# Gate and up of a SwiGLU feed-forward in seven half-size products instead of eight, with two accumulator tiles read in turn

## The chip, the cores and the metric

One core of one Trainium2 chip. Its engines run side by side, each with a queue of its own that is worked off in order: TensorE (PE; PEld is its weight load), VectorE (DVE), ScalarE (ACT), GpSimd (POOL) and SyncE (SP, which here issues most transfers). TensorE writes its sums into PSUM, of which the feed-forward uses four tiles of two banks in turn; everything else lies in SBUF. The metric is the device time of one execution in microseconds; less is better.

## The reference

One inference step of a small decoder trunk: a Conformer convolution layer, then a layer of dilated sliding-window attention, each followed by a SwiGLU feed-forward, for 512 prompt columns and 64 sample columns. The change concerns the feed-forward, which is computed twice:

```python
def swiglu(x, g, w_gate_up, w_down):
    gu = rms_norm(x, g) @ w_gate_up
    return (jax.nn.silu(gu[..., :D_FF]) * gu[..., D_FF:]) @ w_down
```

D_MODEL is 1024 (8 tiles of 128), D_FF is 2816 (22 blocks of 128). All values are fp32.

## The kernel before

Activations stand transposed: 128 partitions hold a tile of the model dimension, and the N = 576 columns are the tokens. A matmul takes a column half of 288 (HN). To keep fp32 accuracy, each operand is split into a high part (rounded, format fp32r) and a low part (the rest), and each product of two tiles is three matmuls: high by high, high by low, low by high (`mm3`, L227 to L230).

`ffn` (L772) works in two halves of 11 blocks. For each block f it computes gate and up: `proj` (L274) runs 8 tiles of the model dimension x 2 column halves x 3 matmuls for gate (48 matmuls) and the same for up, so 96 in a block, into one PSUM tile each. Behind it DVE multiplies with the row scale rs (L795), ACT takes silu (L797), DVE multiplies up with rs (L799) and with the gate (L800), and the result is split into hh (ACT, L271) and hl (DVE, L272). After 11 blocks come the down products of that half: 8 output tiles with 11 x 2 x 3 = 66 matmuls each, which DVE adds into the residual xT (L810). The very first block computes gate and up as a `pair` (L284), which alternates between two PSUM tiles every three matmuls, because its input arrives tile by tile.

Weights stream in: `w_load` (L110) issues the transfer of a block's weights (1 MB for gate and up) from SP into one of two raw buffers; `w_split` (L130) makes high (ACT, L140) and low parts (DVE, L141) into one of two pairs of buffers whi and wlo; `w_next` (L161) hands out what is ready, loads the block after next and splits the next. `bg_copy` (L180) issues at each `w_next`, on the same SP queue, one or two background copies of 1 MB from cache to output. The order of all instructions is the program's own: each engine works them off as they were written, and semaphores hold back what isn't ready. After the first feed-forward, `x_fill` (L848) prepares the attention's input behind each of the last down products; after the second, `y_rows` (L1546) transposes and writes the output.

Of the kernel before, what the change touches and what calls it, by code (L numbers as in the profile page):

```python
# [44 lines left out]
GH = 3072  # L45
DFF = 2816
FT = DFF // 128
TAPS = 31
EPS = 1e-6
SC = HD ** -0.5  # L50
# [40 lines left out]
def trunk(ctx: ExitStack, tc: tile.TileContext, I, O, dbg=None):  # L91
# [12 lines left out]
    def spec(ap, shape, scale=None):  # L104
        specs.append((ap, shape, scale))

    wstate = {"raw": [], "ready": [], "n": 0, "rate": 1.5, "lo": nc.vector, "cut": 4}
    BUFR, BUFH = 2, 2

    def w_load():  # L110
        if not specs:
            return
        ap, shape, scale = specs.pop(0)
        raw = wpool.tile([128, WSLOT], F32, tag="wraw", name="wraw", bufs=BUFR)
        n = int(np.prod(shape))
        v = raw[:, :n]
        if len(shape) == 2:
            v = v.rearrange("p (a b) -> p a b", a=shape[0])
        else:
            v = v.rearrange("p (a b c) -> p a b c", a=shape[0], b=shape[1])  # L120
        if len(shape) == 2:
            nc.sync.dma_start(v, ap)
        else:
            for j in range(shape[1]):
                nc.sync.dma_start(v[:, :, j], ap[j])
        wstate["raw"].append((raw, n, shape, scale))

    parts = []

    def w_split(cut=None):  # L130
# [5 lines left out]
        hi = wpool.tile([128, WSLOT], F32R, tag="whi", name="whi", bufs=BUFH)  # L136
        lo = wpool.tile([128, WSLOT], F32R, tag="wlo", name="wlo", bufs=BUFH)

        def plain(c):
            nc.scalar.activation(hi[:, c], raw[:, c], AF.Copy)  # L140
            wstate["lo"].tensor_sub(lo[:, c], raw[:, c], hi[:, c].bitcast(F32))  # L141

        def scaled(k, m):
            c = slice(k * m, (k + 1) * m)
            nc.scalar.activation(hi[:, c], raw[:, c], AF.Copy, scale=scale[:, k:k + 1])
            nc.vector.scalar_tensor_tensor(lo[:, c], raw[:, c], scale[:, k:k + 1],
                                           hi[:, c].bitcast(F32), op0=ALU.mult, op1=ALU.subtract)

        if scale is None:
            parts.extend(partial(plain, slice(i * n // cut, (i + 1) * n // cut)) for i in range(cut))  # L150
        else:
            parts.extend(partial(scaled, k, n // shape[0]) for k in range(shape[0]))
        pat = "p (a b) -> p a b" if len(shape) == 2 else "p (a b c) -> p a b c"
        kw = dict(a=shape[0]) if len(shape) == 2 else dict(a=shape[0], b=shape[1])
        wstate["ready"].append((hi[:, :n].rearrange(pat, **kw), lo[:, :n].rearrange(pat, **kw)))

    def w_work(n=100):
        for _ in range(min(n, len(parts))):
            parts.pop(0)()

    def w_next(lazy=False):  # L161
        w_work()
# [32 lines left out]

    def ffn_specs(l):
        wg, wd = I["w_gate_up"][l], I["w_down"][l]
        for hf in range(2):
            for f in range(hf * 11, hf * 11 + 11):
                spec([col_blocks(wg, 0, KT, f * 128, 128), col_blocks(wg, 0, KT, DFF + f * 128, 128)], (KT, 2, 128))  # L200
            for m in range(KT):
                spec(col_blocks(wd, hf * 11, 11, m * 128, 128), (11, 128))

    ffn_specs(0)

# [75 lines left out]
                    j == 0, j == len(ks) - 1)  # L281
        return pt[:, :, :HN]

    def pair(ps, wh, wl, xh, xl):  # L284

        pts = [ps.tile([128, 2, 512], F32, tag="mm", name="pmp") for _ in range(2)]
        for k in range(KT):
            for h in range(2):
                c = slice(h * HN, (h + 1) * HN)
                for i in range(2):  # L290
                    mm3(pts[i][:, h, :HN], wh[i][:, k], wl[i][:, k], xh[:, k, c], xl[:, k, c], k == 0, k == KT - 1)
        return pts

    def cut2(w):
# [477 lines left out]
    def ffn(l, u, before_last, after, late=0):  # L772
        with ExitStack() as cx:
            big = cx.enter_context(tc.tile_pool(name=f"f_big{l}", bufs=1))
            wk = cx.enter_context(tc.tile_pool(name=f"f_wk{l}", bufs=2))
            ps = cx.enter_context(tc.tile_pool(name=f"f_ps{l}", bufs=4, space=PSUM, reuse_waits="tile"))
            rs = big.tile([128, N], F32, name="rs")
            hh = big.tile([128, 11, N], F32R, name="hh")
            hl = big.tile([128, 11, N], F32R, name="hl")
            ks = [(k, k) for k in range(KT)]  # L780
            for hf in range(2):
                for f in range(11):
                    wh, wl = w_next()
                    if hf == 0 and f == 0:

                        pg, pu = (x[:, :, :HN] for x in pair(ps, [wh[:, :, i] for i in range(2)],
                                                             [wl[:, :, i] for i in range(2)], u.uh, u.ul))
                    else:
                        pg = proj(ps, wh, wl, u.uh, u.ul, ks, lambda w, k: w[:, k, 0])
                        pu = proj(ps, wh, wl, u.uh, u.ul, ks, lambda w, k: w[:, k, 1])  # L790
                    if hf == 0 and f == 0:
                        rstd_bc(ps, wk, u.acc, rs)
                        nc.scalar.activation(u.acc[:, 0:1], u.acc[:, 0:1], AF.Silu)
                    t = wk.tile([128, N], F32, name="gt")
                    nc.vector.tensor_mul(halves(t), pg, halves(rs))  # L795
                    s = wk.tile([128, N], F32, name="sg")
                    nc.scalar.activation(s, t, AF.Silu)  # L797
                    t2 = wk.tile([128, N], F32, name="gt2")
                    nc.vector.tensor_mul(halves(t2), pu, halves(rs))  # L799
                    nc.vector.tensor_mul(t2, t2, s)  # L800
                    split(hh[:, f], hl[:, f], t2)
                if hf:
                    u.close()
                    before_last()
                for m in range(KT):
                    wh, wl = w_next()
                    pt = proj(ps, wh, wl, hh, hl, [(k, k) for k in range(11)], lambda w, k: w[:, k])
                    if hf and late and m:
                        after(ps, wk, m - 1)
                    nc.vector.tensor_add(halves(xT[:, m]), halves(xT[:, m]), pt)  # L810
                    if hf and not late:
                        after(ps, wk, m)
                if hf and late:
                    after(ps, wk, KT - 1)


# [780 lines left out]
```

## Time and profile before

| | |
|---|---|
| Median of 3 runs (lowest, highest) | 2047.7 us (2044.57, 2049.89) |
| The profiled execution: its time | 2048.85 us |
| Its span, and its granted TensorE clock | 2047.1 us, 0.983 |
| TensorE matmul busy | 1948.9 us (95%), 17109 records |
| DVE, ACT, POOL busy | 1013.2, 810.2, 158.8 us |
| First feed-forward | about 305 to 718 us |
| Second feed-forward | about 1625 to 2041 us |
| Main transfer queue | 384.06 MB, 62.7% of 16 engines |

How to read it: a row of instructions names the line, the engine, the operation, output<-inputs and the shape; then the count, the busy time, the mean length of one and the idle time in front of them with what ended it. Matmuls overlap in TensorE's pipeline, so the length of one is more than their distance. A window's row gives each engine's busy time and count in that stretch, then the granted clock, the share of the transfer engines and GB/s.

### The profile page before, as it was taken

What the parts mean: (1) busy time and instruction counts of PE and PEld (TensorE: products, weight loads), DVE (VectorE), ACT (ScalarE), POOL (GpSimd) and SP (SyncE); (2) the same over time, 40 slices, a digit from 0 to 9 for tenths busy, and PEclk for the clock granted to TensorE, in tenths of its full rate; (3) what the DMA queues carried; (4) which work ended last, traced back from release to release, by engine and by line L of the source; (5) the groups of instructions that cost most, each with busy time, mean ns of one, the idle gap of its engine ahead of it and who ended that gap; (6) DMA issues with size and microseconds to landing.
All of it is one profiled execution on the core that took longest, in us unless ns stands there. A gap on an engine that the chain in (4) does not pass through costs nothing.

```text
span 2047.1 us, 40767 instructions
## 1 busy us (share of the span) xinstructions
PE 1948.9 (95%) x17109; PEld 1799.7 (88%) x17109; DVE 1013.2 (49%) x1922; ACT 810.2 (40%) x1836; POOL 158.8 (8%) x292
## 2 busy tenths in 40 slices
PE   6989699999999999999999999989988999999998
PEld 6767499999999999988888888877667999999998
DVE  5766674433343477356356445524556444334432
ACT  6554643221222344444244434437764332112221
POOL 1000000000000033032022012200113000000000
PEclk9999799999999999999999999999988999999999
DMA  7440086658665866787986986989686665633222
GB/s 212 144 145 23 23 295 217 225 210 279 206 205 185 294 207 181 238 233 192 252 226 187 258 253 198 217 213 229 176 191 214 208 209 199 234 97 83 77 72 75
DMA packets 368874, 387.82 MB, mean 189 GB/s; under 512 B 17983, under 2 KB 357975, under 8 KB 367010
## 3 DMA queue, kind: packets, MB, share of 16 engines
q1 hardware_dynamic: 368130, 384.06, 62.7%
q8 instruction: 135, 2.21, 0.5%
q0 software_dynamic: 560, 1.14, 0.2%
q14 instruction: 49, 0.40, 0.1%
HBM read 348.07 MB, written 146.86 MB: 242 GB/s over the span
## 4 chain that ended last, share of the span: by engine, by line
PE 88%; ACT 4%; DVE 3%; DMA 3%; issue 1%; SPq 1%; another core or an unknown queue 0%; ACTq 0%; DVEq 0%
PE pmm L230 13%; PE pmm L229 13%; PE pmm L228 13%; PE pj L228 7%; PE pj L229 7%; PE pj L230 7%; PE pj L1192 3%; PE tp L965 3%; PE acc L558 3%; PE pmp L229 2%; PE pmp L230 2%; PE pmp L228 2%; PE pv L1063 2%; PE tp L990 2%; ACT prod L588 1%; PE sc L1328 1%
## 5 line engine op out<-in xcount | busy, mean ns | idle before, releaser
L230 PE MATMUL pmm<-uh,wlo 128*128 128x288 f32 x1344 | 396.2, 295 | 0.0
L228 PE MATMUL pmm<-uh,whi 128*128 128x288 f32 x1344 | 395.9, 295 | 0.0
L229 PE MATMUL pmm<-ul,whi 128*128 128x288 f32 x1344 | 395.8, 294 | 0.0
L228 PE MATMUL pj<-whi,xh 128*128 128x256 f32 x1152 | 332.8, 289 | 0.9 <-DVE xT L810 0.9
L229 PE MATMUL pj<-wlo,xh 128*128 128x256 f32 x1152 | 321.8, 279 | 0.0
L230 PE MATMUL pj<-whi,xl 128*128 128x256 f32 x1152 | 321.8, 279 | 0.0
L228 PEld LDWEIGHTS pmm<-uh,whi 128*128 128x128 f32 x1344 | 252.1, 188 | 0.1
L229 PEld LDWEIGHTS pmm<-ul,whi 128*128 128x128 f32 x1344 | 252.1, 188 | 0.1
L230 PEld LDWEIGHTS pmm<-uh,wlo 128*128 128x128 f32 x1344 | 252.1, 188 | 0.0
L228 PEld LDWEIGHTS pj<-whi,xh 128*128 128x128 f32 x1152 | 216.3, 188 | 11.4 <-issue 10.8
L140 ACT ACTIVATE whi<-wraw 128x1024 fp32r<-128x1024 f32 (+3 forms) x206 | 169.2, 871 | 123.1 <-PE pmm L229 100.6
L229 PEld LDWEIGHTS pj<-wlo,xh 128*128 128x128 f32 x1152 | 216.5, 188 | 0.0
L230 PEld LDWEIGHTS pj<-whi,xl 128*128 128x128 f32 x1152 | 216.0, 187 | 0.0
L141 DVE TENSOR_TENSOR wlo<-wraw,whi 128x1024 fp32r<-128x1024 f32 (+3 forms) x206 | 197.7, 1003 | 23.7 <-ACT whi L140 23.4
L228 PE MATMUL pmm<-hh,whi 128*128 128x288 f32 x704 | 207.6, 295 | 0.0
L230 PE MATMUL pmm<-hh,wlo 128*128 128x288 f32 x704 | 207.5, 295 | 0.0
L229 PE MATMUL pmm<-hl,whi 128*128 128x288 f32 x704 | 207.2, 294 | 0.0
L799 DVE TENSOR_TENSOR gt<-pmm,rs 128x576 f32<-128x576 f32 x42 | 31.8, 757 | 224.6 <-PE pmm L230 224.6
L271 ACT ACTIVATE hh<-gt 128x576 fp32r<-128x576 f32 x44 | 30.2, 686 | 263.3 <-DVE gt L800 263.3
L229 PEld LDWEIGHTS pmm<-hl,whi 128*128 128x128 f32 x704 | 132.1, 188 | 0.0
L228 PEld LDWEIGHTS pmm<-hh,whi 128*128 128x128 f32 x704 | 132.1, 188 | 0.0
L230 PEld LDWEIGHTS pmm<-hh,wlo 128*128 128x128 f32 x704 | 132.0, 188 | 0.0
(295 smaller groups left out, 3516.4 us busy)
## 6 DMA issues: line engine op xcount, KB each, us to landing
out_dram<-in_cache_kv_w_dram SPq DMA_DIRECT2D x64, 1016.0 KB
wraw<-in_w_gate_up_dram SPq DMA_DIRECT2D x88, 512.0 KB
out_dram<-in_cache_kv_w_dram SPq DMA_DIRECT2D x32, 1008.0 KB
wraw<-in_w_kv_dram SPq DMA_DIRECT2D x24, 1024.0 KB
wraw<-in_w_down_dram SPq DMA_DIRECT2D x32, 704.0 KB
kk<-in_cache_kv_w_dram SPq DMA_DIRECT2D x40, 512.0 KB
vv<-in_cache_kv_w_dram SPq DMA_DIRECT2D x40, 512.0 KB
scr<-r SPq DMA_DIRECT2D x36, 512.0 KB
```

Of the source, the lines that this page charges most:

```text
L140: nc.scalar.activation(hi[:, c], raw[:, c], AF.Copy)
L141: wstate["lo"].tensor_sub(lo[:, c], raw[:, c], hi[:, c].bitcast(F32))
L228: nc.tensor.matmul(out, wh, xh, start=start, stop=False)
L229: nc.tensor.matmul(out, wh, xl, start=False, stop=False)
L230: nc.tensor.matmul(out, wl, xh, start=False, stop=stop)
L271: nc.scalar.activation(hi, x, AF.Copy)
L558: nc.tensor.matmul(acc[r][32 * (j - m):32 * (j - m) + 32], DG[c][g, j], exf[c][g, j:S + j], start=m == 0, stop=j + 4 >= TAPS)
L799: nc.vector.tensor_mul(halves(t2), pu, halves(rs))
L965: nc.tensor.transpose(pt[:, j * 128:(j + 1) * 128], Z["k", n][:, j, i * 128:(i + 1) * 128], ident)
L990: nc.tensor.matmul(pt[32 * bi:32 * bi + 32, a:a + n], q[:, x, i, b], kn[:, x, i, T * b:T * b + T] if k is None else k[:, i, bi], start=i = ...
L1063: nc.tensor.matmul(pvt[r], ph[:n, ti, r], v[:n, bi], start=i == 0, stop=i == 9)
L1192: nc.tensor.matmul(pt[:, :CW], xs[:, k], x[:, k], start=k == 0 and x is wh, stop=k == KT - 1 and x is wl)
```

## The change

The inner dimension (8 tiles) is halved, the 576 columns are halved, and gate and up are the two halves of the output: a 2 x 2 by 2 x 2 block product. Before, it takes 8 half-size products (4 tiles x 3 = 12 matmuls each); Winograd's form of Strassen's scheme needs 7, at the price of sums of the weights (four, `sw`), sums of the inputs (four, `th` and `tl`) and sums of the results.

- The 22 blocks are worked in quarters of 5, 6, 6 and 5 (`QUARTERS`). The first quarter stays as it was (`plain`, L869), since the row scale rs is known only after its first block. Since gate and up columns of both halves are mixed, the inputs must carry rs beforehand: `input_sums` (L844) makes the four scaled sums behind blocks 1 to 4, and `rescale` (L857) rewrites the parts of uh and ul that are used directly, during the first quarter's down products.
- In the other 17 blocks `seven` (L891) issues the seven products into two PSUM tiles: pwa (one bank, a) and pwc (two banks, c and b), in the order a, c, a, b, a, c, a. Several products add onto what stands in the bank; in between ACT copies the bank's state (p1, p5, u2, u3) or DVE reads it, while the next product goes to the other tile.
- The weights of such a block are seven parts of 512 columns, in two buffers of whi and wlo: r0, r1 and two sums, then two sums and r3. `w_split` queues the four sums (DVE, L193), then two splits of 1024 columns (L314, L315); `w_tail` (L134) makes the rest, after the block that uses the second buffer has ended. The raw buffer is free only after that.
- The down products come after each quarter, with 5 or 6 tiles inside, in pairs of output tiles (640 or 768 columns of weights a part); the first pair of each quarter runs as `pair`.

The core of the diff:

```diff
+QUARTERS = [(0, 5), (5, 6), (11, 6), (17, 5)]
...
+    def w_tail():
...
+            split(hi[:, :1024], lo[:, :1024], sw[:, 1024:])
+            split(hi[:, 1024:1536], lo[:, 1024:1536], raw[:, 1536:])
...
+            parts.extend([partial(add, t[0], r[2], r[3]), partial(sub, t[1], t[0], r[0]), partial(sub, t[2], r[0], r[2]),
+                          partial(sub, t[3], r[1], t[1]), direct, summed])
...
+            def input_sums(j):
...
+                nc.vector.tensor_sub(t[:, 0], za[:, h1], za[:, h0])
+                nc.vector.tensor_sub(t[:, 1], zb[:, h1], t[:, 0])
+                nc.vector.tensor_sub(t[:, 2], zb[:, h1], za[:, h1])
+                nc.vector.tensor_sub(t[:, 3], zb[:, h0], t[:, 1])
+                nc.scalar.activation(th[:, :, j], t, AF.Copy)
...
+            def seven(i):
+
+                wxh, wxl, wyh, wyl = w_take()
+                pa = ps.tile([128, 2, 512], F32, tag="mm", name="pwa")
+                pc = ps.tile([128, 2, 512], F32, tag="mm", name="pwc")
+                a, b, c = pa[:, 0, :HN], pc[:, 1, :HN], pc[:, 0, :HN]
...
+                direct(a, wxh, wxl, 0, 0, h0, True)
+                nc.scalar.activation(sn["p1"], a, AF.Copy)
+                summed(c, wxh, wxl, 2, 0, True)
+                nc.scalar.activation(sn["p5"], c, AF.Copy)
+                if sums_next:
+                    w_split()
+                    w_work(4)
+                summed(a, wxh, wxl, 3, 1, False)
+                nc.scalar.activation(sn["u2"], a, AF.Copy)
+                direct(b, wxh, wxl, 1, 4, h0, True)
+                nc.vector.tensor_add(s[:, h0], sn["p1"], b)
+                flush()
+                if not sums_next:
+                    w_split()
+                w_work(1)
+                nc.scalar.activation(s[:, h0], s[:, h0], AF.Silu)
+                summed(a, wyh, wyl, 0, 2, False)
+                nc.scalar.activation(sn["u3"], a, AF.Copy)
+                nc.vector.tensor_add(t2[:, h1], sn["u3"], sn["p5"])
+                w_work()
+                direct(c, wyh, wyl, 1, 4, h1, False)
+                nc.vector.tensor_add(s[:, h1], sn["u2"], c)
+                nc.scalar.activation(s[:, h1], s[:, h1], AF.Silu)
+                summed(a, wyh, wyl, 2, 3, False)
+                nc.vector.tensor_mul(t2[:, h1], t2[:, h1], s[:, h1])
+                nc.vector.tensor_mul(t2[:, h0], s[:, h0], a)
+                w_tail()
+                nc.scalar.activation(hh[:, i], t2, AF.Copy)
+                pend.append(lambda: nc.vector.tensor_sub(hl[:, i], t2, hh[:, i].bitcast(F32)))
+                if not sums_next:
+                    flush()
```

**DVE in one gate block.** Before, of one block in the second half of the first feed-forward (a gt with a number is the product of gate and up):

```order
L795 TENSOR_TENSOR gt<-pmm,rs 128x576
L799 TENSOR_TENSOR gt_5282<-pmm,rs 128x576
L800 TENSOR_TENSOR gt_5282<-gt_5282,sg 128x576
L272 TENSOR_TENSOR hl<-gt_5282,hh 128x576
L141 TENSOR_TENSOR wlo<-wraw,whi 128x1024 x2
```

Now, of one half-size block (p and u with numbers are ACT's copies; two of the four weight sums of line 193 stand ahead of the first row):

```order
L193 TENSOR_TENSOR sw<-wraw 128x512
L193 TENSOR_TENSOR sw<-wraw,sw 128x512
L925 TENSOR_TENSOR sg<-p_4736,pwc 128x288
L943 TENSOR_TENSOR hl<-gt_4615,hh 128x576
L315 TENSOR_TENSOR wlo<-wraw,whi 128x1024
L933 TENSOR_TENSOR gt_4741<-u_4739,p_4737 128x288
L315 TENSOR_TENSOR wlo<-sw,whi 128x1024
L936 TENSOR_TENSOR sg<-u_4738,pwc 128x288
L939 TENSOR_TENSOR gt_4741<-gt_4741,sg 128x288
L940 TENSOR_TENSOR gt_4741<-sg,pwa 128x288
L315 TENSOR_TENSOR wlo<-sw,whi 128x1024
L315 TENSOR_TENSOR wlo<-wraw,whi 128x512
```

Six operations have become fourteen, weight work and results are interleaved, and hl of a block has moved into the next.

**ACT in the gate blocks.** Before, from the last blocks of a half into its down products:

```order
L140 ACTIVATE whi<-wraw 128x1024 x2
L797 ACTIVATE sg<-gt 128x576
L271 ACTIVATE hh<-gt_4426 128x576
L140 ACTIVATE whi<-wraw 128x704 x2
L797 ACTIVATE sg<-gt 128x576
L271 ACTIVATE hh<-gt_4542 128x576
L140 ACTIVATE whi<-wraw 128x704 x14
```

Now, of one half-size block:

```order
L916 ACTIVATE p_4736<-pwa 128x288
L918 ACTIVATE p_4737<-pwc 128x288
L923 ACTIVATE u_4738<-pwa 128x288
L314 ACTIVATE whi<-wraw 128x1024
L930 ACTIVATE sg<-sg 128x288
L932 ACTIVATE u_4739<-pwa 128x288
L314 ACTIVATE whi<-sw 128x1024
L937 ACTIVATE sg<-sg 128x288
L314 ACTIVATE whi<-sw 128x1024
L314 ACTIVATE whi<-wraw 128x512
L942 ACTIVATE hh<-gt_4741 128x576
```

Four copies out of PSUM are new, each between two products of the same bank, and the next block's first copy stands behind the last splits and hh.

**ACT at the end of the first quarter**, from its last gate block into the down products, now:

```order
L883 ACTIVATE sg<-sg 128x576
L314 ACTIVATE hh<-gt_3870 128x576
L854 ACTIVATE th<-sw 128x4x288
L174 ACTIVATE whi<-wraw 128x640 x2
L863 ACTIVATE uh<-zs 128x288 x2
L174 ACTIVATE whi<-wraw 128x640 x2
L863 ACTIVATE uh<-zs 128x288 x2
```

Against the rows of before, th stands between hh and the weights of the next down products, and the rescaling (uh) between those of the later ones.

On TensorE the built program has 14727 matmuls in place of 15135; the number of transfers is the same (807).

More of the change, by code (lines that the diff above doesn't have):

```diff
@@ L123, in w_load, with w_slot @@
         else:
-            for j in range(shape[1]):
-                nc.sync.dma_start(v[:, :, j], ap[j])
+            for j, a in enumerate(ap):
+                nc.sync.dma_start(v[:, j] if shape[0] == 2 else v[:, :, j], a)
         wstate["raw"].append((raw, n, shape, scale))
     parts = []
+    def w_slot():
+        return [wpool.tile([128, WSLOT], F32R, tag=t, name=t, bufs=BUFH) for t in ("whi", "wlo")]
+    def w_tail():
+        if wstate["tail"] is not None:
+            w_work()
+            raw, sw, e = wstate["tail"]
+            wstate["tail"] = None
+            hi, lo = w_slot()
+            split(hi[:, :1024], lo[:, :1024], sw[:, 1024:])
+            split(hi[:, 1024:1536], lo[:, 1024:1536], raw[:, 1536:])
+            e += [hi, lo]
     def w_split(cut=None):
@@ L135, in w_split, with direct, summed @@
         raw, n, shape, scale = wstate["raw"].pop(0)
-        hi = wpool.tile([128, WSLOT], F32R, tag="whi", name="whi", bufs=BUFH)
-        lo = wpool.tile([128, WSLOT], F32R, tag="wlo", name="wlo", bufs=BUFH)
+        if scale == "seven":
+            r = [raw[:, i * 512:(i + 1) * 512] for i in range(4)]
+            sw = wstate["sums"]()
+            t = [sw[:, i * 512:(i + 1) * 512] for i in range(4)]
+            add, sub = nc.vector.tensor_add, nc.vector.tensor_sub
+            e = []
+            def direct():
+                e.extend(w_slot())
+                split(e[0][:, :1024], e[1][:, :1024], raw[:, :1024])
+            def summed():
+                split(e[0][:, 1024:], e[1][:, 1024:], sw[:, :1024])
+            parts.extend([partial(add, t[0], r[2], r[3]), partial(sub, t[1], t[0], r[0]), partial(sub, t[2], r[0], r[2]),
+                          partial(sub, t[3], r[1], t[1]), direct, summed])
+            wstate["tail"] = (raw, sw, e)
+            wstate["ready"].append(e)
+            return
+        hi, lo = w_slot()
         def plain(c):
@@ L780, in ffn @@
+            th = tp.tile([128, 4, 4, HN], F32R, name="th")
+            tl = tp.tile([128, 4, 4, HN], F32R, name="tl")
             ks = [(k, k) for k in range(KT)]
[L781 to L787, printed above, removed]
-                    else:
[L789 to L802, printed above, removed]
@@ L806, in ffn @@
                     wh, wl = w_next()
[L807 to L813, printed above, removed]
+                    flush()
+                    if not q:
+                        rescale([[0, 1], [2, 3, 4], [5, 6, 7], []][m0 // 2])
@@ new lines, in ffn @@
+                    pts = None if m0 else pair(ps, cut2(wh), cut2(wl), hh, hl, nf)
+                    for m in (m0, m0 + 1):
+                        pt = pts[m][:, :, :HN] if pts else proj(
+                            ps, wh, wl, hh, hl, [(k, k) for k in range(nf)],
+                            lambda w, k: w[:, k, 128 * (m - m0):128 * (m - m0) + 128])
+                        if last and late and m:
+                            after(ps, wk, m - 1)
+                        nc.vector.tensor_add(halves(xT[:, m]), halves(xT[:, m]), pt)
+                        if last and not late:
+                            after(ps, wk, m)
@@ L814, in ffn @@
+                    w_tail()
+                if last and late:
                     after(ps, wk, KT - 1)
```

103 lines of the change are left out of this document (91 added, 12 removed).

## The prediction

> **What bounds the kernel now.** I read the page's busy times first, then the waits of TensorE inside the two feed-forward stages, then windows inside them.
>
> ```profile
> span 2047.1 us, 40767 instructions
> PE 1948.9 (95%) x17109; PEld 1799.7 (88%) x17109; DVE 1013.2 (49%) x1922; ACT 810.2 (40%) x1836; POOL 158.8 (8%) x292
> ```
>
> TensorE (PE) is busy 95% of the span. Where the change is made it is busy without a gap. In the waits from 300 to 725 us (the first feed-forward) and from 1620 us to the end (the second), TensorE has one row each:
>
> ```profile
> PE pj L228 <- DVE xT L810: 0.9, 1, 0.9
> ...
> PE ptr L1550 <- DVE xT L810: 0.3, 1, 0.3
> ```
>
> Total, times, longest: 0.9 and 0.3 us, both behind the stages' last products. One window in gate blocks, and the stretch before the feed-forward, whose paired products switch banks every three matmuls:
>
> ```profile
> 340.00:430.00 90.00, 90.00 (x681) 90.00 (x680) 38.89 (x44) 22.90 (x29) 0.00 (x0) 1.00 0.56 191
> 262.00:306.00 44.00, 44.00 (x334) 44.00 (x333) 33.90 (x50) 17.45 (x23) 0.00 (x0) 1.00 0.93 325
> ```
>
> Columns: length, busy time and count of PE, PEld, DVE, ACT, POOL, granted clock, DMA share, GB/s. 90.00/681 is 132.2 ns per matmul, and 44.00/334 is 131.7 ns while banks alternate: switching banks costs nothing. The page's 295 ns of one matmul is its length in the pipeline, not its pace. Two successive gate blocks end their up product here:
>
> ```profile
> 1954.57 0.76 DVE L799 TENSOR_TENSOR gt<-pmm,rs 128x576 f32<-128x576 f32 x1 [5.60 <-PE pmm L230]
> ...
> 1967.29 0.76 DVE L799 TENSOR_TENSOR gt<-pmm,rs 128x576 f32<-128x576 f32 x1 [5.60 <-PE pmm L230]
> ```
>
> 12.72 us for 96 matmuls, 132.5 ns each, waits on finished work included. So the stage's time is its matmul count, and a matmul that goes is worth 132.4 ns, as long as nothing else becomes late.
>
> **The change: what goes.** 17 of 22 blocks in each of two layers issue 84 matmuls in place of 96: 34 x 12 = 408 fewer, 408 x 0.1324 = 54.0 us. A block becomes 7 products of 12 matmuls, 1.59 us each, 11.13 us in all. The down products keep their number (22 x 48 in each layer).
>
> **What is added, and whether it hides.** The rows that price it:
>
> ```profile
> L141 DVE TENSOR_TENSOR wlo<-wraw,whi 128x1024 fp32r<-128x1024 f32 x102 | 120.4, 1222 | 11.6 <-ACT whi L140 11.3
> L140 ACT ACTIVATE whi<-wraw 128x1024 fp32r<-128x1024 f32 x102 | 101.7, 1044 | 28.8 <-PE pmm L229 28.0 <-DMA wraw<-in_a_w_out_dram 0.8
> L141 DVE TENSOR_TENSOR wlo<-wraw,whi 128x512 fp32r<-128x512 f32 x32 | 19.9, 684 | 2.4 <-ACT whi L140 2.4
> L140 ACT ACTIVATE whi<-wraw 128x512 fp32r<-128x512 f32 x32 | 17.4, 616 | 0.0
> L1152 ACT ACTIVATE t<-pj 128x512 f32<-128x512 f32 x48 | 28.7, 597 | 123.3 <-PE pj L230 123.2
> L272 DVE TENSOR_TENSOR hl<-gt,hh 128x576 fp32r<-128x576 f32 x44 | 33.3, 758 | 33.1 <-ACT hh L271 33.1
> L271 ACT ACTIVATE hh<-gt 128x576 fp32r<-128x576 f32 x44 | 30.2, 686 | 263.3 <-DVE gt L800 263.3
> L810 DVE TENSOR_TENSOR xT<-xT,pmm 128x576 f32<-128x576 f32 x32 | 24.1, 754 | 173.6 <-PE pmm L230 173.6
> L268 DVE SCALAR_TENSOR_TENSOR ul<-xT,cols,uh 128x576 fp32r<-128x576 f32 x16 | 13.1, 818 | 13.5 <-ACT uh L267 13.5
> ```
>
> From the widths 512 and 1024, DVE takes 146 ns + 1.05 ns a column and ACT 188 ns + 0.84 ns; no row is 288 wide, so 449 and 429 ns are estimates. PSUM as source changes little (597 against 616; 754 against 758). A half-size block then loads DVE with 4 x 684 (weight sums) + 3 x 1222 + 684 (low parts) + 758 (hl) + 5 x 449 = 10.1 us of 11.13, where a block of before has about 5.4 of 12.72; ACT with 3 x 1044 + 616 + 686 + 6 x 429 = 7.0 us. DVE at 91% in a fixed order is the danger, so I lay one steady block out. Hand-overs:
>
> ```profile
> 318.08 0.76 DVE L795 TENSOR_TENSOR gt<-pmp,rs 128x576 f32<-128x576 f32 x1
> 318.76 0.75 DVE L799 TENSOR_TENSOR gt<-pmp,rs 128x576 f32<-128x576 f32 x1
> 319.61 0.76 DVE L800 TENSOR_TENSOR gt<-gt,sg 128x576 f32<-128x576 f32 x1
> 321.12 0.76 DVE L272 TENSOR_TENSOR hl<-gt,hh 128x576 fp32r<-128x576 f32 x1 [0.75 <-ACT hh L271]
> ...
> 320.40 0.69 ACT L271 ACTIVATE hh<-gt 128x576 fp32r<-128x576 f32 x1 [0.84 <-DVE gt L800]
> ```
>
> DVE to ACT to DVE costs 0.03 us a hand-over (319.61 + 0.76 to 320.40; 320.40 + 0.69 to 321.12); two DVE operations without a wait overlap by 0.08 (318.08 + 0.76 against 318.76). With the products' results at 1.75, 3.34, 4.93, 6.52, 8.11, 9.70 and 11.29 us (issue end plus 295 - 132 ns), each queue in its order gives, once it repeats:
>
> ```
> ACT  p1 2.43-2.86  p5 3.38-3.81  u2 4.97-5.40  whi 6.56-7.61  silu 7.51-7.94  u3 8.15-8.58
>      whi(sums) 8.48-9.53  silu 11.20-11.63  whi(tail) 11.53-13.09  hh 12.99-13.66  next p1 13.56-13.99
> DVE  sums 3.24-5.75  add 6.56-7.01  hl 6.93-7.69  wlo 7.65-8.87  add 8.80-9.24  wlo(sums) 9.57-10.79
>      add 10.71-11.16  mul 11.67-12.12  mul 12.04-12.49  wlo(tail) 12.61-14.45  next sums 14.37
> ```
>
> The next block's third product adds onto the bank that p1 copies, and would start at 11.13 + 3.18 = 14.31: the copy ends 0.32 us before. All else is earlier (wlo 8.87 and 10.79 against uses at 11.4 and 13.0). So the alternation holds with 0.32 us to spare, and the lane that decides is add, hl, wlo, add, wlo on DVE, then silu, hh and p1 on ACT. If every DVE and ACT operation took 10% longer, the same layout makes the third product wait 0.33 us; at 20%, 0.96. 28 blocks follow a half-size block: 0 to 9.3 us at 0 to 10%. The durations hardly vary, as the 44 executions of one row show (least, median, most):
>
> ```profile
> L272 DVE TENSOR_TENSOR hl<-gt,hh x44: 757/758/760, 321.1 to 1969.7; 128x576 fp32r<-128x576 f32 x44
> ```
>
> No new kind of operation is used, so I take 0.05 a block, 1.4 us. A gain is excluded there: TensorE can't start a product before the one in front of it.
>
> TensorE's own risk is its clock:
>
> ```profile
> 205.00:256.00 51.00, 35.63 (x406) 23.37 (x405) 33.08 (x49) 34.12 (x79) 0.00 (x0) 0.80 0.07 23
> 1050.00:1200.00 150.00, 146.53 (x1392) 129.69 (x1393) 77.23 (x170) 63.89 (x151) 25.25 (x52) 1.00 0.85 230
> ```
>
> Idle for 15 us of 51 it is granted 0.80; idle in many pieces for 3.5 us of 150 it keeps 1.00. My layout is nearer the second, so I take 1.00.
> The Trainium skill, TensorE: Matmul & The Clock Gate, section "A second HAM failure mode: psum-queue depth-cycling", speaks against this change: cycling through accumulator banks makes the engine idle briefly between groups so often that the clock swings between half and full. The paired products of 262 to 306 us, at 1.00 with a switch every three matmuls, don't show it; by the rule the sum would lose its gain, as the third rival prices.
>
> **First quarter.** Its five blocks keep 96 matmuls, and the sums of the inputs (two at 818, four at 449, a high part 1152 wide at 1.15 and a low at 1.36 us, estimates) fit into 12.72 us, except in the fifth. There ACT's th stands ahead of the high parts of the second pair's weights. After the block's last result: mul, mul, hh, hl to 3.1 us, two scaled inputs to 4.6, four differences to 6.2, th to 7.4, whi (640 wide, 0.72) to 8.0, wlo to 8.9; TensorE has done the first pair (60 x 0.1324) at 7.8 and wants that wlo at 8.05. 0.9 us in each layer, 1.8 in all (0 if th is earlier, 4 if a second pair is held up as well). DVE then lags behind, with the rescaling on top; laid out in the same way, the first half-size block's first low part is ready 31.2 us after that fifth block, and TensorE wants it at 32.8.
>
> **Other boundaries.** Down products in quarters add 32 adds into xT at 754 ns under TensorE's 7.95 or 9.5 us a pair: hidden. At the end of the first feed-forward:
>
> ```profile
> 717.83 0.76 DVE L810 TENSOR_TENSOR xT<-xT,pmm 128x576 f32<-128x576 f32 x1 [2.61 <-PE pmm L230]
> ...
> 720.03 0.75 DVE L264 TENSOR_TENSOR xacc<-xacc,sq 128x576 f32<-128x576 f32 x1
> ...
> 711.96 3.25 DVE L146 SCALAR_TENSOR_TENSOR wlo<-wraw,cols,whi 128x256 fp32r<-128x256 f32 x8
> ```
>
> Each column block needs 2.9 us of DVE (717.83 to 720.78), and now comes every 3.97 us, not 8.7; with the eight parts of the next weights (3.25) that is 9.1 in 7.95, so the last one ends about 0.5 us later (0 to 2.5, if the weights land late).
>
> **Transfers.** SP's queue, and the windows it fills:
>
> ```profile
> 628.19 0.37 SPq L122 DMA_DIRECT2D wraw<-in_w_down_dram  x1
> 628.61 1.35 SPq L184 DMA_DIRECT2D out_dram<-in_cache_kv_w_dram  x2
> ...
> 628.20:636.00 7.80, 7.80 (x61) 7.80 (x60) 1.51 (x2) 0.69 (x1) 0.00 (x0) 1.00 0.98 359
> 636.00:640.00 4.00, 4.00 (x32) 4.00 (x31) 3.14 (x4) 2.05 (x3) 0.00 (x0) 1.00 0.02 4
> ```
>
> A load and two copies, 2.8 MB, are through 7.8 us after issue. A gate block's load with two copies is 3.1 MB, 8.7 us at 359 GB/s. It is issued when the tail's wlo frees the buffer (14.45) and used by the sums one block later (25.5): 11.1 us. Hidden, with 2.4 us over.
>
> **Sum.** The profiled execution took 2048.85 us (1.75 outside the span). 2048.85 - 54.0 + 1.8 + 0.5 + 1.4 = 1998.55. The median of the runs, 2047.7, is 1.15 below it: 1997.4.
>
> **The rivals.**
> - **DVE's lane is late** (chance 0.24). For: 91% occupancy, 0.32 us to spare, estimates at width 288. Against: the spare survives 5%. At 10 to 20% longer operations, 9 to 27 us come back: 2005 to 2023. Hand-overs of 0.2 us, not 0.03, cost 0.43 a block, 12 us; at 0.4 (1.57 a block) the gain is gone. I leave 0.02 for no change and 0.03 for slower in it.
> - **Weights land late** in the first feed-forward (0.05). If copies go ahead of the load and the pace is the 297 GB/s of its busier stretches, 10.5 us plus the issue reaches the 11.1; 1 us in some 14 blocks is 2011. Row:
>
> ```profile
> 655.00:715.00 60.00, 60.00 (x456) 60.00 (x455) 27.74 (x47) 20.85 (x41) 0.00 (x0) 1.00 0.85 297
> ```
>
> - **The clock falls** (0.06, slower). Short waits at each switch take the granted clock down in the gate blocks. At 0.80 a block takes 11.13/0.80 = 13.9 us, 1.2 more than 12.72: 34 x 1.2 = 41 us, 2089. It decides below 0.875 (11.13/12.72). Against: 1.00 in the window from 1050. This is what the rule of the Trainium skill above would do here.
>
> That the change doesn't take the matmuls out is excluded: the built order has 408 fewer.
>
> **Chances and range.** Forecast 0.65: between 2047.7 - 54.0 less some 3 us of spread between runs (1991) and all upper bounds (2007). Faster by over 0.3% (6 us, what a measurement here can tell): 0.65 + 0.19 + 0.05 = 0.89; within: 0.02; slower: 0.03 + 0.06 = 0.09. The range 1990 to 2025 takes in the first two rivals up to 20% longer operations, and leaves out some 0.05 below and 0.12 above.
>
> **What would show it.** 11.1 to 11.2 us from one hh to the next in half-size blocks; TensorE's waits on p1 absent or under 0.1 us; clock 1.00; a wait of about 0.9 us on wlo at each second pair of the first quarter. Blocks over 11.5 us with TensorE waiting for ACT's p1 or DVE's wlo would prove the first rival; waits on wraw the second.

## The result, and the profile after

The changed kernel takes 2000.4 us (median of 4 runs, 1999.1 to 2002.3), the kernel before on the same chip 2048.8 us: a ratio of 0.9768 [0.975, 0.9785], 48 us less. The forecast was 1997.4 us with a range of 1990 to 2025. The profiled execution took 2000.88 us. Its page begins:

```profile
span 1999.1 us, 40703 instructions
...
PE 1896.0 (95%) x16701; PEld 1746.3 (87%) x16701; DVE 1224.9 (61%) x2314; ACT 936.7 (47%) x2098; POOL 157.1 (8%) x292
```

408 matmul records fewer, and TensorE still at 95%: the span fell with TensorE's work. VectorE has 212 us more work than before and ScalarE 126. Whether that stays hidden is read from the waits of TensorE, first from 300 to 720 us, then from 1590 us to the end:

```profile
PE pj L271 <- DVE xT L973: 2.1, 1, 2.1
PE pmm L273 <- DVE wlo L175: 0.3, 1, 0.3
...
PE ptr L1714 <- DVE xT L973: 0.7, 2, 0.4
PE pmm L273 <- DVE wlo L175: 0.3, 1, 0.3
```

In 34 half-size blocks there is no wait at all: no row names pwa or pwc. A window inside them (busy time and count of PE, PEld, DVE, ACT, POOL, then clock, transfer share, GB/s):

```profile
400.00:460.00 60.00, 60.00 (x454) 60.00 (x453) 46.84 (x71) 34.15 (x59) 0.00 (x0) 1.00 0.72 250
```

60.00/454 is 132.2 ns per matmul at a granted clock of 1.00, as before. Where each feed-forward begins and ends is read from TensorE's timeline, by the start of its first product behind the first pair, and of the first attention product or the last down product:

```profile
310.68 0.51 PE L271 MATMUL pmm<-uh,whi 128*128 128x288 f32 x1
...
694.86 0.36 PE L271 MATMUL pj<-whi,xh 128*128 128x256 f32 x1 [2.12 <-DVE xT L973]
...
1606.53 0.51 PE L271 MATMUL pmm<-uh,whi 128*128 128x288 f32 x1
...
1992.21 0.30 PE L273 MATMUL pmm<-hh,wlo 128*128 128x288 f32 x1
```

The same rows of the kernel before:

```profile
310.45 0.51 PE L228 MATMUL pmm<-uh,whi 128*128 128x288 f32 x1
...
718.73 0.35 PE L228 MATMUL pj<-whi,xh 128*128 128x256 f32 x1 [0.94 <-DVE xT L810]
...
1629.82 0.51 PE L228 MATMUL pmm<-uh,whi 128*128 128x288 f32 x1
...
2040.18 0.29 PE L230 MATMUL pmm<-hh,wlo 128*128 128x288 f32 x1
```

The first feed-forward went from 408.28 to 384.18 us, the second from 410.36 to 385.68: 24.1 and 24.7 us less, of the 27.0 that 204 matmuls make. Nearly all of the 48 us lies there; between the two, 911.1 us became 911.7. The losses are 2.9 and 2.3 us, and the timeline shows where.

**A block.** The first and the last of five successive hh on ACT:

```profile
407.60 0.67 ACT L942 ACTIVATE hh<-gt 128x576 fp32r<-128x576 f32 x1
...
452.25 0.67 ACT L942 ACTIVATE hh<-gt 128x576 fp32r<-128x576 f32 x1
```

44.65 us for four blocks: 11.16 us each, laid out at 11.13. Inside one block, ACT's end of the lane, then the first matmul of the third product:

```profile
429.93 0.67 ACT L942 ACTIVATE hh<-gt 128x576 fp32r<-128x576 f32 x1
430.50 0.39 ACT L916 ACTIVATE p<-pwa 128x288 f32<-128x288 f32 x1
...
431.27 0.30 PE L905 MATMUL pwa<-th,whi 128*128 128x288 f32 x1
```

The copy p1 ends at 430.89, 0.38 us before TensorE starts onto that bank, where the layout had 0.32. Where TensorE does wait for p1 (the run without the last product, below), it starts 0.06 us after the copy's end; with that hand-over, which the layout had left out, 0.32 us are to spare. DVE's idle times in the same block, the figure in brackets:

```profile
428.58 0.46 DVE L939 TENSOR_TENSOR gt<-gt,sg 128x288 f32<-128x288 f32 x1 [0.51 <-ACT sg L937]
...
434.72 0.45 DVE L925 TENSOR_TENSOR sg<-p,pwc 128x288 f32<-128x288 f32 x1 [0.83 <-PE pwc L905]
...
437.64 1.23 DVE L315 TENSOR_TENSOR wlo<-sw,whi 128x1024 fp32r<-128x1024 f32 x1 [0.29 <-ACT whi L314]
```

1.63 us idle in 11.16, so 9.5 us of DVE's time are taken. The prediction's 10.1 us is a sum of durations, which counts twice the parts in which two operations overlap.

**The first quarter.** The second pair of down products, on ACT, DVE and PE:

```profile
368.19 1.17 ACT L854 ACTIVATE th<-sw 128x1152 fp32r<-128x1152 f32 x1 [3.88 <-DVE sw L853]
369.27 1.35 ACT L174 ACTIVATE whi<-wraw 128x640 fp32r<-128x640 f32 x2
...
369.60 0.29 PE L273 MATMUL pmp<-hh,wlo 128*128 128x288 f32 x1
...
370.02 1.56 DVE L175 TENSOR_TENSOR wlo<-wraw,whi 128x640 fp32r<-128x640 f32 x2 [1.86 <-ACT whi L174]
...
370.04 0.40 PE L271 MATMUL pmm<-hh,whi 128*128 128x288 f32 x1
370.27 0.30 PE L272 MATMUL pmm<-hl,whi 128*128 128x288 f32 x1
370.90 0.40 PE L273 MATMUL pmm<-hh,wlo 128*128 128x288 f32 x1 [0.33 <-DVE wlo L175]
371.13 0.29 PE L271 MATMUL pmm<-hh,whi 128*128 128x288 f32 x1
```

th stands in front of the weights' high parts, and TensorE stops twice, for whi at 370.04 and for wlo at 370.90. From 369.60 to 371.13 are four steps, 1.53 us where 4 x 0.132 would be 0.53: 1.0 us lost, of which the view of waits names 0.33.

**The end of the first feed-forward**, DVE's rows and TensorE's last down product:

```profile
687.93 3.25 DVE L180 SCALAR_TENSOR_TENSOR wlo<-wraw,cols,whi 128x256 fp32r<-128x256 f32 x8
...
692.44 0.29 PE L273 MATMUL pmm<-hh,wlo 128*128 128x288 f32 x1
...
693.96 0.75 DVE L973 TENSOR_TENSOR xT<-xT,pmm 128x576 f32<-128x576 f32 x1
```

The last add has no bracket: DVE was busy up to it. The product's result was there at 692.73, 1.2 us earlier. TensorE waits 2.1 us for that add, against 0.9 before: 1.2 us lost.

**The end of the second feed-forward.** The transposes of the output stand between the last down products, and the first of them waits for an add into xT:

```profile
1964.42 0.29 PE L273 MATMUL pmp<-hh,wlo 128*128 128x288 f32 x1
1965.16 0.66 PE L1714 MATMUL ptr<-ident,xT 128*128 128x128 f32 x4 [0.45 <-DVE xT L973]
```

From one to the other are 0.74 us; before, such a step took 0.14 (1984.43 to 1984.57 us). With the 0.06 us that these transposes take longer behind the stop, 0.66 us are lost. The other 0.30 of the 0.7 us in the view lies behind the last down product, as it did before.

### The profile page after: what moved, and what is told of

Read it like the earlier page. It is cut to its first block, busy times and chain, and to the rows that moved or that the text cites. A ratio compares the mean times of both kernels' runs of the same rounds, so it can differ in the third digit from the quotient of the medians.

```text
span 1999.1 us, 40703 instructions
## 1 busy us (share of the span) xinstructions
PE 1896.0 (95%) x16701; PEld 1746.3 (87%) x16701; DVE 1224.9 (61%) x2314; ACT 936.7 (47%) x2098; POOL 157.1 (8%) x292
## 4 chain that ended last, share of the span: by engine, by line
PE 85%; DVE 5%; ACT 5%; DMA 4%; issue 1%; SPq 1%; another core or an unknown queue 0%; ACTq 0%; DVEq 0%
PE pwa L905 11%; PE pwc L905 8%; PE pj L271 7%; PE pj L272 7%; PE pj L273 7%; PE pmm L273 5%; PE pmm L272 5%; PE pmm L271 5%; PE pj L1356 3%; PE tp L1129 3%; PE pmp L272 3%; PE pmp L273 3%; PE pmp L271 3%; PE acc L601 3%; PE tp L1154 2%; PE pv L1227 2%
## 5 line engine op out<-in xcount | busy, mean ns | idle before, releaser
L273 PE MATMUL pmm<-hh,wlo 128*128 128x288 f32 x528 | 155.8, 295 | 0.7 <-DVE wlo L175 0.7
L175 DVE TENSOR_TENSOR wlo<-wraw,whi 128x512 fp32r<-128x512 f32 (+4 forms) x138 | 118.0, 896 | 30.4 <-ACT whi L174 30.1
L174 ACT ACTIVATE whi<-wraw 128x512 fp32r<-128x512 f32 (+4 forms) x138 | 102.0, 786 | 72.5 <-PE pmm L272 31.7
L180 DVE SCALAR_TENSOR_TENSOR wlo<-wraw,cols,whi 128x256 fp32r<-128x256 f32 x288 | 120.4, 477 | 18.8 <-ACT whi L179 18.8
L179 ACT ACTIVATE whi<-wraw,cols 128x256 fp32r<-128x256 f32 x288 | 124.2, 499 | 0.2 <-DMA wraw<-in_w_q_dram 0.2
L905 PE MATMUL pwa<-th,whi 128*128 128x288 f32 x408 | 120.7, 296 | 0.0
L905 PE MATMUL pwa<-tl,whi 128*128 128x288 f32 x408 | 120.4, 295 | 0.0
L905 PE MATMUL pwa<-th,wlo 128*128 128x288 f32 x408 | 120.0, 294 | 0.0
L1129 PE MATMUL tp<-ident,kk 128*128 128x128 f32 x576 | 89.5, 281 | 15.1 <-ACT kt L1138 6.2
L1138 ACT ACTIVATE kt<-tp 128x512 f32<-128x512 f32 x128 | 74.8, 593 | 59.1 <-PE tp L1129 58.5
```

What stands on the lines that cost most here:

```text
L273: nc.tensor.matmul(out, wl, xh, start=False, stop=stop)
L905: nc.tensor.matmul(out, x[:, w], y(j), start=start and j + n == 0, stop=j == 3 and n == 2, skip_group_check=True)
L1129: nc.tensor.transpose(pt[:, j * 128:(j + 1) * 128], Z["k", n][:, j, i * 128:(i + 1) * 128], ident)
L1138: nc.scalar.activation(kt[:, i, bi] if g else kt[:, i].rearrange("p b c -> p (b c)"), Z["tp"], AF.Copy)
```

## The experiments

The theory: TensorE's number of matmuls sets the time, and the half-size form's added work is hidden as long as the next product's tile is free in time. The lane, that is the chain add, hl, wlo, add, wlo on VectorE and then silu, hh, p1 on ScalarE, has 0.3 us to spare there. The rivals: part of the gain is the quartering's; alternation doesn't matter, only the count does; VectorE's load is what is nearly full, wherever its work stands. Each kernel ran beside the kernel before on the same chip, and the ratios are to that. "Feed-forwards" below is the sum of the two lengths measured as above: 818.64 us before, 769.86 after, and 770.39 in a second profile of the same changed kernel.

**The changed kernel again**, beside other runs.

> The changed kernel once more, for the runs beside it: 1999 to 2004 us; the two feed-forwards as in its first profile, to 0.2 us; what differs lies in the convolution and the attention, which all these kernels have in common.

Measured: 2003.2 us (1998.7 to 2006.0), ratio 0.9775 [0.9755, 0.9794]. The feed-forwards are 0.5 us longer, not within 0.2: the wait on xT at the end of the first is 2.6 us in place of 2.1. Between them are 913.9 us in place of 911.7. Two or three microseconds of a total are no difference between kernels here.

**Quarters alone.**

```diff
-                     "seven" if f0 else None)
+                     None)
...
-                    if q:
-                        seven(i)
-                    else:
-                        plain(i)
+                    plain(f0 + i, i)
```

The sums of the inputs and the rescaling are left out with it.

> The quarters alone: all 22 blocks keep 96 matmuls, the down products come after quarters of 5, 6, 6 and 5 blocks and in pairs of output tiles; no half-size products, no sums of inputs or weights. The theory (the matmul count sets the time, and quartering hides): no gain, 2047 to 2051 us, against 2048.8 before; a loss of 0 to 2 us from the end of the first feed-forward. The rival (part of the gain comes from the smaller stages or the weights' new layout): under 2043 us.

> The quarters alone once more: its first profile (2050.7 us) had the two feed-forwards 1.5 and 0.8 us longer than before, its unprofiled runs were at 2057. If the quarters cost only what the profile shows, 2049 to 2053 us in the median; if the unprofiled runs are right, 2055 to 2059 us again.

Measured: 2057.2 us, ratio 1.0044 [1.0028, 1.0061], and the second time 2055.7 us, 1.0026 [1.0009, 1.0043]. No gain comes from the quarters; they cost 5 to 9 us in the medians, more than I expected. The feed-forwards account for 2.4 us (821.01) and 2.7 us (821.35), at their ends: TensorE's waits on xT are 2.2 and 0.7 us there, as in the changed kernel. In the second profile (2055.96 us) most of the rest lies in the attention, whose code is the same: 915.1 us for 911.1. The first profile (2050.72 us) was the shortest of its four executions and doesn't show the rest. The attention's length differs between all these profiles, and whether this part is the quarters' doing stays open. From quarters to the changed kernel the feed-forwards lose 821.01 - 769.86 = 51.2 us: the half-size products carry the whole gain.

**An eighth product.**

```diff
+                direct(b, wxh, wxl, 1, 4, h0, True)
                 direct(b, wxh, wxl, 1, 4, h0, True)
```

> The product on bank b is issued twice (12 matmuls more in each half-size block, the second starts the bank anew, so the result stays): 96 matmuls in a block as in the kernel before, with all sums, copies and reads of the half-size form. The theory (a matmul costs 132.4 ns, the rest hides): 408 x 0.1324 = 54 us over the changed kernel, 2053 to 2056 us, with all of VectorE's and ScalarE's added work under it. The rival (the gain comes in part from something else than the count, the quarters or the new layout of the weights): under 2048 us.

Measured: 2053.9 us, ratio 1.0019 [1.0007, 1.0031]. Its feed-forwards take 823.72 us, 53.9 us over the changed kernel, 132 ns for each of 408 matmuls. With the count of before, all of the half-size form's added work costs 823.72 - 821.01 = 2.7 us over the quarters alone. The count is the gain.

**Two products of one bank in succession.**

```diff
-                direct(c, wyh, wyl, 1, 4, h1, False)
-                nc.vector.tensor_add(s[:, h1], sn["u2"], c)
-                nc.scalar.activation(s[:, h1], s[:, h1], AF.Silu)
                 summed(a, wyh, wyl, 2, 3, False)
-                nc.vector.tensor_mul(t2[:, h1], t2[:, h1], s[:, h1])
                 nc.vector.tensor_mul(t2[:, h0], s[:, h0], a)
+                direct(c, wyh, wyl, 1, 4, h1, False)
+                nc.vector.tensor_add(s[:, h1], sn["u2"], c)
+                nc.scalar.activation(s[:, h1], s[:, h1], AF.Silu)
+                nc.vector.tensor_mul(t2[:, h1], t2[:, h1], s[:, h1])
```

> In each half-size block the last two products change places, so that two products on the bank a follow each other: a, c, a, b, a, a, c in place of a, c, a, b, a, c, a. The number of matmuls stays. The theory: TensorE can start the second of the two only when ACT has copied the first's result: 0.16 us until the result is there, 0.43 for the copy, 0.06 for two hand-overs, 0.65 us in each of 34 blocks, and since gate's second half now ends last and starts the lane to p1, up to 0.3 more at p1 in 28 of them: 22 to 33 us, 2022 to 2033 us, and TensorE's waits name ACT's u3. The rival (only the count matters, the reads are short enough): 2000 to 2003 us.

Measured: 2043.4 us, ratio 0.9972 [0.996, 0.9983]. Its waits from 300 to 735 us:

```profile
PE pwa L905 <- ACT u L932: 8.5, 17, 0.5
PE pwa L905 <- ACT p L916: 2.6, 14, 0.2
```

The median of nine executions lies 10 us above the expected 2022 to 2033. The profiled one took 2037.4 us, the shortest of the nine, so some 6 us of the median are not in what follows.

Only the order differs, and 38 of the 49 us in the feed-forwards are gone (808.15 us). The waits are where the theory put them, u3 in all 17 blocks and p1 in 14 of each layer (the second layer has the same two rows), but they sum to 2 x 11.1 = 22 us, not 38. One of them on TensorE's timeline shows what the view leaves out:

```profile
412.80 0.29 PE L905 MATMUL pwa<-th,wlo 128*128 128x288 f32 x1
413.60 0.40 PE L905 MATMUL pwa<-th,whi 128*128 128x288 f32 x1 [0.50 <-ACT u L932]
413.83 0.29 PE L905 MATMUL pwa<-tl,whi 128*128 128x288 f32 x1
```

From 412.80 to 413.60 is 0.80 us, 0.67 more than a step of 0.13, as expected; the matmul behind the stop takes 0.10 more (0.23 to the next). The view counts only the 0.50 from the modelled end of the last matmul. So a stop costs 0.27 more than its row names, 17 us for 62 stops: with the 22 that makes the 38. The expectation had the 0.17, not the 0.10, which is what its upper bound of 33 lacks. "Only the count matters" is refuted, for the waits stand where the order was changed.

**The same work on VectorE at two places.** Two idle additions behind the weight sums, or ahead of the add for gate's second half:

```diff
+                def more():
+                    if sums_next:
+                        for k in range(2):
+                            z = big.tile([128, 512], F32, tag="zz", name="zz")
+                            nc.vector.tensor_add(z, xT[:, k, :512], xT[:, k + 2, :512])
...
                     w_work(4)
+                more()
```

and for the second kernel

```diff
                 w_work()
+                more()
                 direct(c, wyh, wyl, 1, 4, h1, False)
```

> Two idle additions of 512 columns on VectorE (1.29 us together) in 28 of the half-size blocks, right behind the four sums of the weights, ahead of the lane add, hl, wlo, add, wlo. The theory: VectorE is idle there for 0.83 us and for 0.29 and 0.51 us later in the block, and what is still late is gone before p1: 0, 2000 to 2003 us. The rival (VectorE's load is what is short): the same cost as with the same work later in the block.

> The same two idle additions (1.29 us) in the same 28 blocks, but in the lane: behind the low parts of the weight sums, ahead of the add that gate's second half needs for its silu. The theory: they go down the lane through silu, hh and p1 less the 0.3 to 0.4 us to spare: a block of 12.0 to 12.2 us, 25 to 30 us in all, 2025 to 2030 us, and TensorE waits on ACT's p1. The rival (VectorE has 1.6 us idle in a block, so 1.3 more fits wherever it stands): 2000 to 2003 us at both places.

Measured: early 2002.6 us, ratio 0.9778 [0.976, 0.9796], feed-forwards 769.94 us: nothing. In the lane 2034.9 us, ratio 0.9932 [0.9916, 0.9949], feed-forwards 801.29 us: 31 us for the same instructions. Its wait from 300 to 735 us, then from the timeline two successive hh on ACT and between them DVE's additions with the add behind them:

```profile
PE pwa L905 <- ACT p L922: 11.7, 14, 0.8
```

```profile
407.92 0.67 ACT L949 ACTIVATE hh<-gt 128x576 fp32r<-128x576 f32 x1
...
416.54 1.41 DVE L918 TENSOR_TENSOR zz<-xT 128x512 f32<-128x512 f32 x2
417.87 0.45 DVE L943 TENSOR_TENSOR sg<-u,pwc 128x288 f32<-128x288 f32 x1
...
420.17 0.67 ACT L949 ACTIVATE hh<-gt 128x576 fp32r<-128x576 f32 x1
```

A block takes 12.25 us, 1.09 more, so 30.5 us in 28 blocks. The additions put the add off by 1.33 us (416.54 to 417.87); less the 0.32 to spare and plus the 0.10 of a stop, that is 1.11. The rest of the 31 us, 0.7, is lost at the end of the first feed-forward. The median lies 5 us above the expected 2025 to 2030; of that the profile shows 1.4 us in the feed-forwards and 2.7 in the attention (914.4 us for 911.7). What counts is where in the lane VectorE's work stands, not its load.

**Six products: what lies behind TensorE.** First the fifth product is left out, then, in another kernel, the last (either leaves out a product, so the feed-forward's result is not computed):

```diff
-                summed(a, wyh, wyl, 0, 2, False)
```

```diff
-                summed(a, wyh, wyl, 2, 3, False)
```

> One of the seven products is left out (the fifth, 12 matmuls, so the feed-forward's result is not computed); all operations on VectorE and ScalarE stay, and the order of the tiles still alternates (a, c, a, b, c, a). TensorE then needs 9.54 us for a block, 1.59 less. The theory (the lane of VectorE and ScalarE is the next bound, 0.3 to 0.4 us behind TensorE): a block falls only to 10.5 to 10.8 us, TensorE waits again, mostly on ACT's p1, and the time falls by some 34 x 0.35 to 0.65 us, to 1978 to 1988 us. The rival (TensorE's count sets the time, nothing is near behind it): 34 x 1.59 = 54 us less, 1946 us.

> Six products again, but the last one is left out in place of the fifth (so the feed-forward's result is not computed): the order a, c, a, b, a, c keeps the two tiles in turn, also into the next block, where the run without the fifth had b and c, of one tile, one behind the other. All operations of VectorE and ScalarE stay. TensorE needs 9.54 us for a block. The theory (without the same-tile wait, the lane of VectorE and ScalarE is the next bound): a block of 10.6 to 11.0 us with TensorE waiting on ACT's p1, 0.2 to 0.5 us less than 11.16 in 28 blocks and up to 1.6 less in the 6 others: 1979 to 1989 us. The rival (nothing but the same-tile wait held the first run back): 9.6 us a block, 1946 to 1950 us.

Measured: 1977.7 us without the fifth, ratio 0.9657 [0.9622, 0.9692]. The time is at the lower edge of the expectation (1978), but the wait isn't the expected one:

```profile
PE pwc L905 <- DVE sg L925: 10.5, 17, 0.6
```

Line 925 reads b; its read ends at 411.84 us, and the product onto c begins at 411.90. Without the fifth product, c's second product follows b's directly, and though b and c are two banks, they are one tile of the program, whose write waits for every read of that tile. So this run doesn't tell about the lane; it shows that the tile has to alternate, not only the bank. Hence the second kernel, in which the tiles take turns: 1985.9 us, ratio 0.9696 [0.9676, 0.9716], although it has the same number of matmuls.

```profile
PE pwa L905 <- ACT p L916: 15.5, 14, 1.1
```

```profile
407.45 0.67 ACT L941 ACTIVATE hh<-gt 128x576 fp32r<-128x576 f32 x1
...
451.17 0.67 ACT L941 ACTIVATE hh<-gt 128x576 fp32r<-128x576 f32 x1
```

Four blocks in 43.72 us: 10.93 us a block, with TensorE needing 9.54 and waiting for p1 at the end of the lane. It is as laid out (10.6 to 11.0). In this kernel gate's second half ends last and the lane with it; without the fifth product a block took 10.5 us (hh at 406.83 and, four blocks on, at 449.00), so how near the lane stands depends on which product is missing. In both, 12 matmuls fewer, worth 1.59 us, brought 0.2 to 0.6 us a block: the next limit is close behind TensorE, in one kernel the tile's reads, in the other the lane.

**The ends of the stages.** First both losses at once, then, with the lines on `input_sums` only, the first quarter's alone:

```diff
-                if f:
+                if 0 < f < 4:
                     input_sums(f - 1)
...
-                    wh, wl = w_next()
+                    wh, wl = w_next(n=4 if last and not late and m0 == 6 else 100)
+                    if not q and not m0:
+                        input_sums(3)
                     flush()
...
+                if last and not late:
+                    w_work()
```

> The changed kernel with two moves at its stages' ends. The last sums of the inputs (with th) stand behind the split of the second pair's weights in the first quarter's down products, no longer ahead of it; and half of the first query weights' splits stand behind the last add into xT of the first feed-forward. The theory: the first quarter's wait of 1.04 us goes in both layers, and 1.1 us at the end of the first feed-forward: 3.2 us less, 1996 to 1998 us. The rival (VectorE is behind anyway in the first quarter, so the wait comes back at the first half-size block's weights): no change, 1999 to 2002 us.

> Of the two moves at the stages' ends only the first: the last sums of the inputs behind the split of the second pair's weights, in both layers. The theory (the wait of 1.04 us at the second pair goes, nothing behind it becomes late): each first quarter at 132.6 to 132.8 ns a matmul in place of 136.5 to 137.8, 2.0 us less than the changed kernel beside it in the two feed-forwards; in the median 1 to 3 us less. The rival (VectorE is as late by then as before, so the first half-size block waits instead): no change in the feed-forwards.

Measured: both, 2003.8 us, ratio 0.9783 [0.9767, 0.9799]; the first alone, 2005.2 us, 0.9786 [0.9769, 0.9804]. Both medians miss their expectation: 1996 to 1998 us, and 1 to 3 us under the changed kernel's 2003.2. In neither is the first quarter's wait left, and nothing became late behind it: the feed-forwards take 767.1 us with both and 767.93 with the first alone, 2 to 3 us less than the changed kernel. The second move is worth little: the wait on xT falls from 2.1 to 1.3 us, and a new one of 0.4 us on the moved low parts appears:

```profile
PE pj L271 <- DVE xT L975: 1.3, 1, 1.3
PE pj L272 <- DVE wlo L180: 0.4, 1, 0.4
```

The totals don't show the 2 us, since the stage between the feed-forwards was longer in both runs. In the run with the first move alone:

```profile
695.69 0.36 PE L271 MATMUL pj<-whi,xh 128*128 128x256 f32 x1 [2.19 <-DVE xT L975]
...
1613.05 0.51 PE L271 MATMUL pmm<-uh,whi 128*128 128x288 f32 x1
```

917.4 us (with both moves 916.9) where the changed kernel had 911.7 and 913.9; the edit of the first move touches no instruction of this stage. These are the two longest of fourteen profiles, and both kernels have the first move: that it makes the attention longer is neither shown nor excluded. So the cause of the loss in the first quarter is shown, but no faster kernel.

**Eighteen blocks.** Quarters of 4, 6, 6 and 6, with the sums of the inputs one block earlier (the last ones as in the kernels above) and part of the rescaling on GpSimd:

```diff
-QUARTERS = [(0, 5), (5, 6), (11, 6), (17, 5)]
+QUARTERS = [(0, 4), (4, 6), (10, 6), (16, 6)]
...
-                    normed(z[:, c], k, c)
-                    nc.scalar.activation(u.uh[:, k, c], z[:, c], AF.Copy)
+                    nc.gpsimd.tensor_mul(z[:, c], xT[:, k, c], rs[:, c])
+                    nc.scalar.activation(u.uh[:, k, c], z[:, c], AF.Copy, scale=u.g[:, k:k + 1])
...
-                if f:
-                    input_sums(f - 1)
+                if f < 3:
+                    input_sums(f)
...
+                    if not q and not m0:
+                        input_sums(3)
```

> Quarters of 4, 6, 6 and 6 blocks, so 18 blocks of half-size products in each layer; the first sums of the inputs come behind the very first block, the last ones as in the run beside it; the rescaling's first product goes to GpSimd, its scale to ScalarE. 24 matmuls fewer: 3.2 us; 2.0 us for the sums of the inputs; up to 1 us at the end of the first feed-forward, where the last quarter's pairs now take 9.5 us for 9.1 us of VectorE's work. The theory: VectorE's work in the shortened first quarter (25 us, by its rows, in 25.4 us of TensorE) just fits: 4 to 6 us under the changed kernel, 1994 to 1998 us. The rival (VectorE or GpSimd is late there, and the first half-size block waits for its weights or inputs, 3 us or more in each layer): 1999 to 2005 us, with TensorE's waits at that block.

Measured: 2016.9 us, ratio 0.9843 [0.9825, 0.986], with 24 matmuls fewer than the changed kernel. From 300 to 420 us:

```profile
PE pwa L906 <- DVE wlo L315: 3.4, 1, 3.4
PE pmm L271 <- ACT whi L174: 2.2, 1, 2.2
PE pmm L273 <- DVE wlo L175: 1.6, 3, 0.7
```

The theory's working for the shortened quarter was too kind. The mechanism is the rival's, but the loss is larger than the rival had it, whose range ended at 2005 us: the first half-size block waits 3.4 us for its weights' low parts, and another 2.2 us go to a plain block's high parts, which stand behind the sums that now begin a block earlier. The feed-forwards take 783.09 us, 13.2 more than the changed kernel's where 24 matmuls should make them 3.2 shorter. Of these 16.4 us the waits named in both stages make 11.8 more than in the changed kernel; with 0.27 us for each further stop that is some 14.5, and the rest was not traced.

## Why the prediction was right, point by point

- **What goes: 54.0 us.** Right. 408 matmuls put back cost 53.9 us. The step was TensorE's pace in this stage, 132.4 ns, and it holds with 34 x 7 switches between tiles.
- **The layout of a steady block.** Right in its parts: 11.16 us for 11.13, 0.32 us to spare for p1 (the copy ends 0.38 us ahead, and a hand-over takes 0.06), and the lane named as the one that decides. Work put in that lane comes out at p1 but for the 0.32 us, while the same work ahead of it costs nothing; and with a product fewer TensorE waits for p1, at the pace laid out. The estimates for width 288 hold: DVE's rows are 0.45 to 0.46 us (449 ns) and ACT's 0.39 to 0.45 (429 ns). The term of 0.05 a block was a guess, not a sum; it was in truth 0.03, and not p1's: no wait occurs.
- **The first quarter: 1.8 us.** Mechanism right (without th in front the loss is gone), size 2.0. The sign given for it, a wait of about 0.9 us on wlo, is in the view only as 0.33: TensorE stops for whi first, and part of both stops has no name there.
- **The end of the first feed-forward: 0.5 us.** Right in kind, too small: 1.2 us, and 1.7 in the second profile. 9.1 us of DVE's work against 7.95 of TensorE leave 1.15, and the prediction put down 0.5 without a reason; DVE has no idle time ahead of the last add.
- **Other boundaries: nothing.** Not quite. Inside the end of the second feed-forward a transpose now stops for xT and costs 0.66 us. With 11.16 for 11.13 in 17 blocks (0.5) and the first quarter (1.0), that makes 2.2 of its 2.3 us.
- **The forecast.** 1997.4 against 2000.4 and, the second time, 2003.2. Of the 3.0 us in the first, 1.5 are these terms (losses of 5.2 us for 3.7), 0.8 the stages ahead of and between the feed-forwards (310.45 to 310.68, 911.1 to 911.7). The rest lies in how a profiled execution stands to a median: I took 1.15 us off for it, and here 2000.88 stands against 2000.37. Two sums of the prediction don't come out, and neither touches the forecast: the upper bounds of its terms add up to 2009.5 us, not 2007; and hand-overs of 0.4 us, at 1.57 in 28 blocks, would take 44 us, not the whole gain of 50.
- **The rivals.** DVE's lane wasn't late; that some 0.3 us were all it had, the idle additions show. Weights were never late in these blocks: no wait on wraw. The granted clock in gate blocks stayed at 1.00 (above, 400 to 460 us), even in the run with six products and the tiles in turn, where TensorE stops for about a microsecond in every block:

```profile
400.00:450.00 50.00, 45.57 (x338) 44.62 (x337) 41.47 (x63) 28.38 (x50) 0.00 (x0) 1.00 0.75 261
```

What the Trainium skill, TensorE: Matmul & The Clock Gate, section "A second HAM failure mode: psum-queue depth-cycling", reports of another kernel, that cycling through banks lets the clock swing, is not seen in these windows: the granted clock is 1.00 with short stops and without.

## What to carry to other kernels

Where TensorE is never idle, removing matmuls pays in full (here 53.9 us for 408), provided each result is read while the next product goes to another tile; lay one block out with the durations of similar rows, and look for the one chain whose end TensorE needs first. The share of busy time of a helping engine says little: 1.4 us more on VectorE cost nothing at one place and 1.1 us a block at another. And before taking out still more matmuls, look at what stands next: here a further product of 1.59 us brought 0.2 to 0.6.

## What the runs showed of the hardware

- A stop of TensorE costs 0.27 us more than the view of waits names: 0.17 because a matmul's modelled end lies behind the start of the next by that much (0.29 us long, 0.13 apart), and 0.10 because the first matmul behind a stop is followed only after 0.23 us, not 0.13.
- The attention, whose code is the same in all these kernels, doesn't always take the same time: 911.1 to 917.4 us between the feed-forwards in fourteen profiles. Its last part doesn't run at a granted clock of 1.00: in windows of 50 us from 1300 to 1550 us it was 0.87 to 0.99 in the first profile of the changed kernel and 0.85 to 1.00 in the longest of the fourteen. Whether the clock makes the difference is not shown. A gain of 2 us in a feed-forward doesn't show in the total beside it, so a small change is first judged by the length of its own stage.
